# One tile of layer 1's expert mixer: its u rows gathered, its v products kept dense; gelu of blocks done ahead placed one block later

## The chip, the cores and the metric

One core of a Trainium2 chip runs the kernel. The metric is the device time of one execution in microseconds (us), from the first to the last instruction and the little that lies around them; less is better. PE is the matrix engine (TensorE), PEld its weight loads, DVE VectorE, ACT ScalarE, POOL GpSimd; SP issues most of the DMAs, ACT and POOL some. Each engine takes its instructions in the order in which they stand.

## What is computed

Two layers over 512 latent tokens and 256 context tokens of 1024 numbers. Each layer has a token mixer (state space in layer 0, attention in layer 1) and then a PEER mixer. Layer 1 gives results for the 512 latent tokens alone. The change is about PEER:

```
def peer_route(t, w_q, keys):
    q = (t @ w_q).reshape(n_tok, PEER_HEADS, 2, PEER_DK // 2)
    s = einsum('thsd,hsnd->thsn', q, keys)
    sv, si = top_k(s, PEER_TOPK)
    cand = sv[:, :, 0, :, None] + sv[:, :, 1, None, :]
    cv, ci = top_k(cand.reshape(...), PEER_TOPK)
    ...
    return e.reshape(n_tok, -1), softmax(cv).reshape(n_tok, -1)

act = gelu(einsum('td,tkd->tk', hb, u_tab[ib])) * gb
out = einsum('tk,tkd->td', act, v_tab[ib])
```

So each token picks 8 x 16 = 128 of 16384 experts; for each picked expert it takes the product with a row of u, a gelu, a gate, and adds that multiple of a row of v.

## The kernel before

Tokens lie in tiles of 128: tiles 0 and 1 are context, 2 to 5 are latent. There are two ways to do PEER for a tile.

**Gathered** (`gather`): for each of the 128 picks, POOL gathers one row of peer_u per token into a `row` buffer [128, 1024] (five buffers, so up to four fetched ahead), and DVE multiplies it by the token and sums (`row<-row,m`, a row sum). After 128 rows ACT does the gelu, DVE multiplies by the gates, and 128 rows of peer_v follow, each added by DVE to f (an f row).

**Dense**: all 16384 experts in 128 blocks of 128, for all tokens of the dense tiles at once. Per block: U is loaded, split into high and low parts (`Uh` by ACT, `Ul` by DVE), 24 u products give s_ps (block's experts x tokens), ACT applies the gelu (`ge`), DVE multiplies by the gate matrix of the block (`Gt`), the result is split into A, and 18 v products (three tiles) add A times the split block of peer_v (`W`, `Wh`, `Wl`) to accumulators held in PSUM. Gate matrices are built first: `gate_matrix` makes one-hot pairs e and o on DVE and ACT for 8 tokens at a time, PE multiplies them (g_ps), ACT copies the products into `stage`, and slabs go to memory (`gm`), from which `Gt` is loaded for 8 blocks at once.

In layer 0 the tiles 2 to 5 are dense and 0, 1 gathered. In layer 1 the tiles 4, 2, 3 are dense and tile 5 is gathered: 384 columns in each u product, three tiles in the v products (`dense_held`).

Some blocks' u part is done ahead, while tokens are still routed (`ahead`): 40 blocks in layer 0, 48 in layer 1 (three of every eight). Their gelu goes to memory (`ged`) and comes back in the dense stretch.

The order comes from generators that `merge` takes turns with by a count of estimated time (`yield` gives it: 5.2 * NT / 4 for a block, R1 = 3.0 for a row of layer 1), and from a scheduler underneath that may move instructions on an engine. Main streams of a `merge` end it; those in `side=` go on later. In layer 1 one `merge` runs output projection, queries and routing, with the work ahead and the gate matrices at its side; then `peer` merges the rest of the gate matrices and the work ahead with the gather at its side; then `dense_held` with the gather. `keep_in_program_order` pins an instruction. `spare` is the pool of the W buffers. Names in the prediction: m is the tile's tokens, idx its picks, rt the routing result, act the 128 activations per token.

## Time and profile before

| what | us |
|---|---|
| median of 3 runs (4092.92 to 4105.87) | 4102.02 |
| the profiled execution, whole time | 4107.66 |
| the profiled execution, span from first to last instruction | 4105.9 |
| PE busy in the span | 3719.0 |
| DVE busy | 3068.7 |
| ACT busy | 1450.2 |
| POOL busy | 1238.6 |

A busy PE is a modelled figure, since matmuls overlap; a pitch (start of one to start of the next) tells more of what a matmul costs. The mean granted clock of TensorE was 0.956 of full speed, two levels taken together. The rows further down come from this one execution.

### The profile page before, as it was taken

What the parts mean: (1) busy time and instruction counts of PE and PEld (TensorE: products, weight loads), DVE (VectorE), ACT (ScalarE), POOL (GpSimd) and SP (SyncE); (2) the same over time, 40 slices, a digit from 0 to 9 for tenths busy, and PEclk for the clock granted to TensorE, in tenths of its full rate; (3) what the DMA queues carried; (4) which work ended last, traced back from release to release, by engine and by line L of the source; (5) the groups of instructions that cost most, each with busy time, mean ns of one, the idle gap of its engine ahead of it and who ended that gap; (6) DMA issues with size and microseconds to landing.
All of it is one profiled execution on the core that took longest, in us unless ns stands there. A gap on an engine that the chain in (4) does not pass through costs nothing.

```text
span 4105.9 us, 52738 instructions
## 1 busy us (share of the span) xinstructions
PE 3719.0 (91%) x18955; PEld 3031.4 (74%) x18955; DVE 3068.7 (75%) x6143; ACT 1450.2 (35%) x2527; POOL 1238.6 (30%) x940
## 2 busy tenths in 40 slices
PE   6759999888689999999999989998887899999998
PEld 3537768677667878778888855568887788888887
DVE  9784387976867788888898844438977677777764
ACT  1321123366632232232332243323466333333332
POOL 5743000022412455556555300000011344444410
PEclk7879999899999999999999999999999999999999
DMA  5457234377888899999999820144477889888873
GB/s 182 134 176 247 80 131 152 96 241 249 293 311 290 291 338 352 337 354 330 342 338 346 301 98 3 44 169 140 123 234 247 317 327 334 318 320 321 328 271 102
DMA packets 380007, 986.06 MB, mean 240 GB/s; under 512 B 64992, under 2 KB 145376, under 8 KB 375136
## 3 DMA queue, kind: packets, MB, share of 16 engines
q1 hardware_dynamic: 198688, 501.34, 35.4%
q0 software_dynamic: 110592, 402.70, 27.4%
q10 hardware_dynamic: 70464, 78.65, 5.5%
q8 instruction: 149, 2.44, 0.2%
q14 instruction: 114, 0.93, 0.1%
HBM read 892.28 MB, written 90.21 MB: 239 GB/s over the span
## 4 chain that ended last, share of the span: by engine, by line
PE 57%; DVE 14%; issue 12%; DMA 7%; POOL 6%; ACT 3%; SPq 0%; POOLq 0%; ACTq 0%; DVEq 0%
PE s_ps L1111 20%; PE acc L1180 8%; PE acc L1255 8%; POOL row L1323 5%; PE qp L920 3%; PE op L791 3%; DMA U<-in_peer_uT 3%; DMA row<-in_peer_v,idx 2%; PE g_ps L1076 2%; PE zp L762 2%; DVE Ul L306 1%; PE op_mla L1560 1%; DVE w L645 1%; PE yp L697 1%; DMA row<-in_peer_u,idx 1%
## 5 line engine op out<-in xcount | busy, mean ns | idle before, releaser
L1111 PE MATMUL s_ps<-Hs,Uh 128*128 128x512 f32 (+1 forms) x4096 | 1187.4, 371 | 13.5 <-ACT Uh L305 13.5
L1323 POOL DMA_INDIRECT row<-in_peer_u,idx x384 | 528.8, 1377 | 2025.2 <-DVE row L1330 1148.2
L1111 PEld LDWEIGHTS s_ps<-Hs,Uh 128*128 128x128 f32 x4096 | 763.1, 190 | 116.2 <-ACT Uh L305 18.7
L1111 PE MATMUL s_ps<-Hs,Ul 128*128 128x512 f32 (+1 forms) x2048 | 759.6, 371 | 27.2 <-DVE Ul L306 27.1
L1255 PE MATMUL acc<-Ws,A 128*128 128x512 f32 x2976 | 689.1, 393 | 37.5 <-ACT A L305 21.4
L1255 PEld LDWEIGHTS acc<-Ws,A 128*128 128x128 f32 x2976 | 564.3, 190 | 160.6 <-ACT A L305 21.9
L1323 POOL DMA_INDIRECT row<-in_peer_v,idx x384 | 502.9, 1310 | 516.8 <-DVE f L1335 460.7
L306 DVE TENSOR_TENSOR Ul<-U,Uh 128x1024 fp32r<-128x1024 f32 x256 | 312.0, 1219 | 281.8 <-ACT Uh L305 273.6
L1335 DVE SCALAR_TENSOR_TENSOR f<-row,act,f 128x1024 f32<-128x1024 f32 x381 | 487.1, 1278 | 33.8 <-DMA row<-in_peer_v,idx 32.2
L1330 DVE SCALAR_TENSOR_TENSOR row<-row,m 128x1024 f32<-128x1024 f32 x384 | 461.0, 1218 | 42.7 <-DMA row<-in_peer_u,idx 41.7
L1111 PEld LDWEIGHTS s_ps<-Hs,Ul 128*128 128x128 f32 x2048 | 389.5, 190 | 82.3 <-DVE Ul L306 35.3
L305 ACT CAST Uh<-U 128x1024 fp32r<-128x1024 f32 x256 | 268.0, 1050 | 500.0 <-DMA U<-in_peer_uT 454.4
L1180 PE MATMUL acc<-Wh,A 128*128 128x512 f32 x1536 | 426.6, 391 | 12.2 <-ACT A L305 12.2
L1076 PE MATMUL g_ps<-o,o 128*128 128x128 f32 x1792 | 240.3, 293 | 114.5 <-ACT o L1059 72.1
L1180 PEld LDWEIGHTS acc<-Wh,A 128*128 128x128 f32 x1536 | 288.3, 188 | 66.7 <-ACT A L305 12.6
L1114 ACT ACTIVATE ge<-s_ps 128x512 f32<-128x512 f32 (+1 forms) x256 | 138.8, 543 | 556.4 <-PE s_ps L1111 551.1
L1076 PEld LDWEIGHTS g_ps<-o,o 128*128 128x128 f32 x1792 | 229.7, 206 | 126.2 <-ACT o L1059 124.5
L305 ACT CAST A<-ge 128x512 fp32r<-128x512 f32 (+1 forms) x256 | 144.6, 565 | 309.0 <-DVE ge L1236 227.1
L305 ACT CAST Ws<-W 128x512 fp32r<-128x512 f32 x256 | 152.1, 619 | 264.3 <-DMA W<-in_peer_v 217.7
L1180 PE MATMUL acc<-Wl,A 128*128 128x512 f32 x768 | 237.5, 390 | 0.0
L306 DVE TENSOR_TENSOR Ws<-W,Ws 128x512 fp32r<-128x512 f32 x256 | 174.3, 684 | 56.0 <-ACT Ws L305 55.7
L306 DVE TENSOR_TENSOR A<-ge,A 128x512 fp32r<-128x512 f32 (+1 forms) x256 | 158.5, 620 | 54.2 <-ACT A L305 53.7
(340 smaller groups left out, 4780.3 us busy)
## 6 DMA issues: line engine op xcount, KB each, us to landing
U<-in_peer_uT SPq DMA_DIRECT2D x256, 512.0 KB
W<-in_peer_v SPq DMA_DIRECT2D x256, 256.0 KB
W<-in_peer_v SPq DMA_DIRECT2D x128, 512.0 KB
gm<-stage ACTq DMA_DIRECT2D x28, 2048.0 KB
ada_wt<-in_ada_w SPq DMA_DIRECT2D x96, 512.0 KB
Gt<-gm SPq DMA_DIRECT2D x16, 2048.0 KB
Gt<-gm SPq DMA_DIRECT2D x16, 1536.0 KB
wq<-in_peer_w_q SPq DMA_DIRECT2D x40, 512.0 KB
```

The lines of the kernel that those rows point to most:

```text
L305: self.nc.scalar.copy(out=hi, in_=x)
L306: lo_eng.tensor_tensor(out=lo, in0=x, in1=hi.bitcast(F32), op=ALU.subtract)
L791: nc.tensor.matmul(out=op, lhsT=y(i, k), rhs=W, start=(k == 0), stop=(k == KD - 1))
L920: PE.matmul(out=st["p"][:, h % 2, i * 128:(i + 1) * 128], lhsT=W[:, k, :], rhs=st[i][:, k, :], start=(k == 0), stop=(k == KD - 1))
L1076: PE.matmul(out=gp[:, t, :], lhsT=o[1][:, t4 * 4 + t, :], rhs=o[0][:, t4 * 4 + t, :], start=True, stop=True)
L1111: PE.matmul(out=sp, lhsT=x[:, k, :], rhs=self.Hs[:, y, k, :], start=(n == 0), stop=(n == 3 * KD - 1))
L1114: S.activation(out=ge, in_=sp, func=AF.Gelu)
L1180: PE.matmul(out=acc[d][hf], lhsT=A[b][:, x, c], rhs=Ws[y][:, hf * 512:(hf + 1) * 512], start=(b == 0 and n == 0), stop=(b == NB - 1 and n ...
L1255: PE.matmul(out=acc[hf][d], lhsT=A[b][:, x, c], rhs=Ws[:, y], start=(j == 0 and n == 0), stop=(j == SB - 1 and n == 2))
L1323: GP.indirect_dma_start(out=r, out_offset=None, in_=tab, in_offset=bass.IndirectOffsetOnAxis(ap=ik[:, k:k + 1], axis=0), element_offset=l ...
L1330: x = V.scalar_tensor_tensor(out=r, in0=r, scalar=1.0, in1=m, op0=ALU.mult, op1=ALU.mult, accum_out=act[:, k:k + 1])
L1335: x = V.scalar_tensor_tensor(out=f, in0=r, scalar=act[:, k:k + 1], in1=f, op0=ALU.mult, op1=ALU.add)
```

## The change

In layer 1, tile 4 becomes half gathered: its picks of peer_u are gathered (128 more row gathers and row sums), its activations go through gelu and gates as for a gathered tile, but instead of gathering rows of v the product takes the gate's place in tile 4's routing result, so that its "gate matrix" holds finished activations. In the dense stretch the u products then cover tiles 2 and 3 alone (`utiles`, 256 columns), and A's part for tile 4 is split straight from Gt. The v products stay at three tiles. Tile 4 is routed first (order 4, 5, 2, 3, before 5, 4, 2, 3), its gate matrix is built last (2, 3, 4, before 4, 2, 3), and the gather is at the side of layer 1's first merge too.

In both layers, the gelu of a block done ahead and its store are issued after the products of the next block (`behind`). The spare pool has four buffers everywhere; in layer 1 it had three. Hs holds the columns of `utiles` alone.

```diff
     def spare(self, shape, name, dt=F32):
-        return self.pool.tile(shape, dt, tag="spare", bufs=max(3, len(self.tiles)), name=name)
+        return self.pool.tile(shape, dt, tag="spare", bufs=4, name=name)
...
-    def peer_setup(self, l, dense, gather):
+    def peer_setup(self, l, dense, gather, half=()):
...
+        self.tiles, self.gathered, self.half = dense, gather, half
+        self.utiles = [ti for ti in dense if ti not in half]
+        self.rts = {}
...
-        self.Hall = self.big([128, 2, KD, T_LAT], "Hs", F32R)
-        self.Hs = self.Hall[:, :, :, T_LAT - len(self.tiles) * 128:]
+        self.Hs = self.big([128, 2, KD, len(self.utiles) * 128], "Hs", F32R)
...
+        if ti in self.half:
+            self.rts[ti] = rt
+            self.gat[ti] = self.m[ti], gate, idx
+            return
...
-        for ti in self.tiles:
+        for ti in self.utiles + list(self.half):
             while ti not in self.routed:
                 yield 1.0
             yield from self.gate_matrix(ti)
...
+        behind = []
+
+        def gelu(n, sp):
+            ge, x = self.dense_ge(sp)
+            self.tc.keep_in_program_order(x)
+            self.nc.scalar.dma_start(out=self.ged[n], in_=ge)
+
         def work(i, Us):
-            self.nc.scalar.dma_start(out=self.ged[i], in_=self.dense_u(Us))
+            behind.append((i, self.dense_s(Us)))
+            if len(behind) > 1:
+                gelu(*behind.pop(0))
             self.n_done = i + 1
             return 5.2 * NT / 4
...
+        gelu(*behind.pop())
...
         def work_u(b, x):
             ge = x if b in self.early else self.dense_u(x)
-            gv = ge.rearrange("p (d g t) -> p d g t", d=NT, g=4)
-            V.tensor_tensor(out=gv, in0=gv, in1=Gt[b // SB][:, :, :, b % SB, :], op=ALU.mult)
+            gv = ge.rearrange("p (d g t) -> p d g t", d=NU, g=4)
+            G = Gt[b // SB][:, :, :, b % SB, :]
+            V.tensor_tensor(out=gv, in0=gv, in1=G[:, NT - NU:], op=ALU.mult)
             A[b] = self.t4([128, 2, TD], "A", F32R)
-            self.split(A[b][:, 0], A[b][:, 1], ge, V)
-            return 0.0 if b in self.early else 5.2 * NT / 4
+            if TG:
+                hi, lo = (A[b][:, x, 0:TG].rearrange("p (d g t) -> p d g t", g=4, t=32) for x in range(2))
+                self.split(hi, lo, G[:, 0:NT - NU], V)
+            self.split(A[b][:, 0, TG:], A[b][:, 1, TG:], ge, V)
+            return 0.0 if b in self.early else 5.2 * NU / 4
...
             for ph, tab in ((0, a["peer_u"]), (1, a["peer_v"])):
+                if ph and ti in self.half:
+                    break
...
-                    V.tensor_tensor(out=act, in0=act, in1=gk, op=ALU.mult)
+                    V.tensor_tensor(out=gk if ti in self.half else act, in0=act, in1=gk, op=ALU.mult)
+            if ti in self.half:
+                self.routed[ti] = self.rts[ti]
+                continue
...
-        order = gather + dense
+        order = gather + [ti for ti in dense if ti not in half]
...
-        merge(scaled(pipeline(steps, LT), FA), chain(*(self.route(ti) for ti in order)), side=(self.aheads, scaled(self.gates, FG1)))
+        merge(scaled(pipeline(steps, LT), FA), chain(*(self.route(ti) for ti in order)),
+              side=(self.gathering, self.aheads, scaled(self.gates, FG1)))
...
-        self.mla([4, 2, 3], [5])
+        self.mla([4, 2, 3], [4, 5], [4])
```

Where the instructions stand, first on DVE at the end of layer 1's gate matrices (e and o are the one-hot pair, `row,act<-row,m` a row sum, Ul and Wl the low parts of a split). Before, up to the first Wl of the dense stretch:

```order
L306 TENSOR_TENSOR Ul<-U,Uh 128x1024
L1054 TENSOR_TENSOR e<-iota_68,iT 128x2048
L1062 TENSOR_TENSOR o_24236<-e,gT 128x768
L1330 SCALAR_TENSOR_TENSOR row,act<-row,m 128x1024
L1054 TENSOR_TENSOR e<-iota_68,iT 128x2048
L1062 TENSOR_TENSOR o_24260<-e,gT 128x768
L1330 SCALAR_TENSOR_TENSOR row,act<-row,m 128x1024 x3
L306 TENSOR_TENSOR Ul<-U,Uh 128x1024
L1330 SCALAR_TENSOR_TENSOR row,act<-row,m 128x1024 x4
L306 TENSOR_TENSOR Wl<-W,Wh 128x1024
```

After, from the last one-hot pair of tile 3 to the first of tile 4 (`rt<-act,rt` puts the finished activations into the routing result):

```order
L1358 SCALAR_TENSOR_TENSOR row,act<-row,m 128x1024
L1060 TENSOR_TENSOR e<-iota_68,iT 128x2048
L1068 TENSOR_TENSOR o_24002<-e,gT 128x768
L1358 SCALAR_TENSOR_TENSOR row,act<-row,m 128x1024 x80
L1370 TENSOR_TENSOR rt<-act,rt 128x128
L1358 SCALAR_TENSOR_TENSOR row,act<-row,m 128x1024
L1060 TENSOR_TENSOR e<-iota_68,iT 128x2048
L1068 TENSOR_TENSOR o_24315<-e,gT 128x768
```

Eighty row sums of tile 4 now stand in one piece between the last pair of tile 3 and the first of tile 4.

Second on ACT in layer 0's work ahead (ge is the gelu of a block, Uh the high part of a later block's split, o the one-hot casts, stage the copies of gate products). Before:

```order
L305 CAST Uh<-U 128x1024
L1080 DMA gm_2818<-stage 128x16x256
L1059 CAST o_6626<-e 128x1024
L1065 ACTIVATE o_6628<-e,gT 128x128 x2
L1114 ACTIVATE ge<-s_ps 128x512
L1078 COPY stage<-g_ps 128x128x4
L1059 CAST o_6646<-e 128x1024
L1065 ACTIVATE o_6648<-e,gT 128x128 x2
L1126 DMA ged_2854<-ge 128x512
```

After, at the same place:

```order
L305 CAST Uh<-U 128x1024
L1114 ACTIVATE ge<-s_ps 128x512
L1086 DMA gm_2818<-stage 128x16x256
L1142 DMA ged_2854<-ge 128x512
L1065 CAST o_6623<-e 128x1024
L1071 ACTIVATE o_6625<-e,gT 128x128 x2
L1065 CAST o_6643<-e 128x1024
L1071 ACTIVATE o_6645<-e,gT 128x128 x2
L1084 COPY stage<-g_ps 128x128x4 x2
```

The gelu moved up behind the cast Uh, and it is now that of the block before; two casts of o follow it ahead of the stage copies.

Third on DVE at the end of the program (`f<-row,act,f` is an f row of tile 5, `f<-acc` the start of a dense tile's epilogue). Before:

```order
L306 TENSOR_TENSOR Wl<-W,Wh 128x1024
L1164 TENSOR_TENSOR ge<-ge,Gt 128x384
L306 TENSOR_TENSOR A<-ge,A 128x384
L1363 TENSOR_TENSOR f<-acc_24477,m_31481 128x512
L1363 TENSOR_TENSOR f<-acc_24478,m_31481 128x512
L1366 SCALAR_TENSOR_TENSOR f<-h,f 128x1024
```

After:

```order
L1187 TENSOR_TENSOR ge<-ge,Gt 128x256
L306 TENSOR_TENSOR A<-ge,A 128x256
L1363 SCALAR_TENSOR_TENSOR f<-row,act,f 128x1024 x10
L1394 TENSOR_TENSOR f<-acc_24829,m_32137 128x512
L1363 SCALAR_TENSOR_TENSOR f<-row,act,f 128x1024
L1394 TENSOR_TENSOR f<-acc_24830,m_32137 128x512
L1396 TENSOR_TENSOR f<-f,m_32108 128x1024
L1397 SCALAR_TENSOR_TENSOR f<-h,f 128x1024 x2
```

The f rows of tile 5 now reach past the last A; in the order before, all of them stand ahead of it.

## Rows read from the trace of the kernel before

**Rows 1.** Busy time by stretch: us, each engine (instructions), PEclk, DMA share, GB/s
```profile
2000.00:2100.00 100.00, 100.00 (x437) 81.71 (x437) 90.79 (x114) 29.09 (x44) 56.82 (x45) 1.00 0.94 337
3700.00:3900.00 200.00, 196.47 (x956) 173.48 (x955) 156.96 (x167) 69.88 (x96) 90.16 (x61) 1.00 0.89 324
```

**Rows 2.** Chain that ended last: start us, us, what (xcount)
```profile
2806.05 12.67 PE s_ps L1111 x72
...
3183.20 15.87 DMA gm<-stage
...
3207.45 6.69 PE acc L1180 x18
...
3471.57 16.34 PE acc L1180 x72
...
4074.70 6.60 PE acc L1180 x29
```

**Rows 3.** Instructions on a tile: ns min/median/max, first and last start
```profile
L306 DVE TENSOR_TENSOR Ul<-U,Uh x48: 1203/1224/1226, 2804.5 to 3184.2; 128x1024 fp32r<-128x1024 f32 x48
...
L1021 DVE TENSOR_TENSOR rt<-oh x8: 279/281/292, 2821.6 to 2989.3; 128x128 f32<-128x128 bf16 x8
...
L1062 DVE TENSOR_TENSOR o<-e,gT x48: 937/958/959, 2875.2 to 3177.7; 128x768 f32<-128x768 bf16 x48
...
L306 DVE TENSOR_TENSOR A<-ge,A x19: 550/557/563, 3960.3 to 4076.4; 128x384 fp32r<-128x384 f32 x19
```

**Rows 4.** Busy time from 2800 to 3000 us, summed
```profile
sum 200.00, PE 169.04 PEld 160.92 DVE 186.46 ACT 91.03 POOL 4.70; mean PE 33.81 PEld 32.18 DVE 37.29 ACT 18.21 POOL 0.94
```

**Rows 5.** Timeline of PE in the attention: start us, us, what
```profile
2563.94 0.29 PE L1536 MATMUL sp_mla<-knT,qnT 128*128 128x256 f32 x1
2564.06 0.28 PE L1537 MATMUL sp_mla<-krT,qs 128*128 128x256 f32 x1
```

**Rows 6.** Timeline of DVE, layer 0's work ahead, its end
```profile
1087.28 1.22 DVE L1054 TENSOR_TENSOR e<-iota,iT 128x2048 bf16<-128x2048 bf16 x1
...
1089.48 1.22 DVE L1330 SCALAR_TENSOR_TENSOR row<-row,m 128x1024 f32<-128x1024 f32 x1
...
1092.82 1.22 DVE L1330 SCALAR_TENSOR_TENSOR row<-row,m 128x1024 f32<-128x1024 f32 x1
...
1120.59 1.23 DVE L1330 SCALAR_TENSOR_TENSOR row<-row,m 128x1024 f32<-128x1024 f32 x1 [0.72 <-DMA row<-in_peer_u,idx]
...
1122.21 1.23 DVE L1330 SCALAR_TENSOR_TENSOR row<-row,m 128x1024 f32<-128x1024 f32 x1 [0.39 <-DMA row<-in_peer_u,idx]
...
1123.83 1.23 DVE L1330 SCALAR_TENSOR_TENSOR row<-row,m 128x1024 f32<-128x1024 f32 x1 [0.39 <-DMA row<-in_peer_u,idx]
```

**Rows 7.** Timeline of DVE, opening of layer 1
```profile
2999.97 1.22 DVE L1330 SCALAR_TENSOR_TENSOR row<-row,m 128x1024 f32<-128x1024 f32 x1
...
3189.88 0.08 DVE L1330 DVE_READ_ACCUMULATOR row<-row,m 128x1 f32 x1
```

**Rows 8.** DMA queue of gathered rows: packets, MB, share of 16 engines
```profile
q0 software_dynamic: 110592, 402.70, 27.4%
```

**Rows 9.** Timeline of POOL, same stretch as rows 6
```profile
1107.68 1.68 POOL L1323 DMA_INDIRECT row<-in_peer_u,idx  x1 [1.67 <-DVE row L1330]
1109.66 0.94 POOL L1323 DMA_INDIRECT row<-in_peer_u,idx  x1 [0.30 <-issue]
1110.91 1.50 POOL L1323 DMA_INDIRECT row<-in_peer_u,idx  x1 [0.30 <-issue]
```

**Rows 10.** Timelines of ACT and PE, layer 0's work ahead; [idle before <-releaser]
```profile
943.59 0.60 ACT L1114 ACTIVATE ge<-s_ps 128x512 f32<-128x512 f32 x1 [4.98 <-PE s_ps L1111]
...
945.69 5.61 PE L1076 MATMUL g_ps<-o,o 128*128 128x128 f32 x32 [2.13 <-ACT o L1059]
```

**Rows 11.** Waits from 660 to 1130 us: us in total, times, longest
```profile
DVE Ul L306 <- ACT Uh L305: 66.2, 19, 9.0
...
PE g_ps L1076 <- ACT o L1059: 44.0, 30, 6.3
```


## What the change does to the time, predicted before it ran

> **What bounds the kernel now.** I read the busy time by stretches first, then the chain that ended last, then the waits. The reader should see three kinds of stretch. From about 3207 us to the end, the stretch that multiplies by peer_v and by peer_u (call it the dense stretch of layer 1), PE is busy 98% of the time with DVE near 78% and DMA at a 0.89 share [rows 1]. PE sets the time there: the chain alternates s_ps pieces (u products) and acc pieces (v products) from 3207.45 to 4081.30 [rows 2], 873.9 us. Between 2804.5 and 2989.5, while tokens are routed (the first Ul row at 2804.5, the last rt row at 2989.3 [rows 3]), DVE is the busiest engine (186.5 of 200 us) and PE is not the limit (169.0) [rows 4]. Between 2989.5 and 3207.45 the gate matrices are built; PE, ACT and DVE wait for each other, and the stretch closes with the write of gm (15.87 us) and the loads behind it [rows 2]. I call the last two stretches together the opening of layer 1. The change takes work from PE in the dense stretch and puts work on DVE in the opening.
>
> **Part 1, narrower u products.** Each of 128 blocks has 24 products of 384 columns; they become 256 columns. The pitch of a 384-column product is 12.67/72 = 0.176 us [rows 2]. A product of this type with 256 columns stands in the attention part: starts 2563.94 and 2564.06, so 0.120 us [rows 5]. 80 of the blocks lie in the dense stretch: 80 x 24 x (0.176 - 0.120) = 107.5 us. The other 48 are done ahead, in the opening; their 48 x 24 x 0.056 = 65 us lie beside DVE, which binds there, and bring nothing. The v products stay: 128 x 18 at 16.34/72 = 0.227 us [rows 2] = 523 us. PE's own sum for the dense stretch goes from 338 + 523 = 861 to 230 + 523 = 753 us. It took 873.9, so 13 us were lost to late inputs. After the change everything else has to come in less time: in bytes 80 u blocks, 128 v blocks and 242 gathered rows of 128 x 1024 floats (0.524 MB each), 16 gate slabs of 1.57 MB and 48 stored gelus of 0.13 MB, together 267 MB; in 773 us that is 346 GB/s. In layer 0 PE stayed 100% busy with DMA at 337 GB/s, a 0.94 share, and DVE at 91 of 100 us [rows 1], so I only raise the loss from 13 to 20 us; the fourth W buffer helps here. Dense stretch: 773 us, **-101 us**. Below nothing this term can't go unless the pitch does not fall.
>
> The Trainium skill (Perfetto Trace Analysis, section Identifying the Most-Contended Engine) judges TensorE's headroom by the share of time that it loads weights rather than by matmul busy time. That share is 173.5 of 200 us here [rows 1], and the change removes no load; by the rule the stretch could not fall below 0.867 x 873.9 = 758 us, 5 us over my 753. The rows at 0.120 us each have a weight load of their own, so the trace does not bear the floor out [rows 5].
>
> **Part 2, 128 more row gathers.** In the order of the changed kernel the row sums of tile 4 stand on DVE as follows: 29 before the routing ends, 19 among the one-hot pairs of tiles 2 and 3, then 80 in an unbroken run, and then the gate matrix of tile 4 with 14 rows of tile 5. During the run nothing is left for PE: all but three blocks of the work ahead are in front of it, and tile 4's gate products need its result. DVE's prices: an e/o pair takes 2.20 us (1087.28 to 1089.48), a pair with a row 3.34 us (1089.48 to 1092.82), so a row costs 1.14 us when it has landed [rows 6]; an Ul reads the same amount as a row, and I take 1.14 for it.
> Routing: 185 us now. Added are 29 rows (33.1) and 13 more Ul that fall here (14.8), and three pairs leave (-6.6): **+41 us**. DVE had 13.5 of 200 us free [rows 4], so 28 to 41.
> From there to the first acc product: 217.9 us now. After: 19 pairs with a row, 7 without, 7 Ul = 87 us of DVE work. In the kernel before, a mixed stretch with 37 pairs, 32 rows and 19 Ul took 190 us (2999.97 to 3189.88 [rows 7]) for a DVE sum of 37 x 2.20 + 51 x 1.14 = 140, 1.36 times as long; pairs and rows without u blocks ran without gaps [rows 6]. With few u blocks in it I take 100 (87 to 118). The run: DMA's price of a row is 0.274 x 4105.9 / 768 = 1.465 us of all 16 engines [rows 8]; POOL could issue one in 1.25 us (1109.66 to 1110.91) [rows 9]; the nearest rows, three row sums with nothing between them, have pitches of 1.62 us, each waiting for its DMA while gm is written [rows 6]. I take 1.5, nearer to DMA's price because gm is soon out of the way: 80 x 1.5 = 120 us (100 to 130). Then 4 us for act, transposes and iT, and 14 x 3.34 + 2 x 2.20 = 51 us. Closing, from the last o row (3177.7 plus 0.96) to the first acc: 29 us, as before [rows 2, 3]. Together 304 against 218: **+86 us**.
>
> **Part 3, the end.** Last A at 4076.4, end at 4105.9 [rows 3]: 29.5 us, in which DVE waits 4.9 us for PE (4081.30) and then does three epilogues in 24.6. In the new order eleven f rows follow the last A (16 us at 1.5 each, in place of the 4.9), then a fourth epilogue, of which I count 8 us (a third of 24.6): **+19 us**. The m5 row is loaded into a buffer that one of the last rows frees; I leave its few us in the range.
>
> **Part 4, gelu behind.** ACT waits for PE before ge, once for 4.98 us, and o casts stand behind it; PE then waits 2.13 us for ACT's o [rows 10]. With the gelu of the block before in that place, ACT does not stop there. This acts in layer 0 (part 2 already counts DVE alone in layer 1). The most that PE can get back directly is its 44.0 us of waits for ACT's o, the most for DVE its 66.2 us of waits for Uh [rows 11]; the least is nothing, since stage copies still wait for products that stand behind s_ps. I take half of the 44: **-20 us**. The wider spare pool costs memory only; in layer 0 it was four already.
>
> **Sum.** Against the profiled execution: 4105.9 - 101 + 41 + 86 + 19 - 20 = 4131 us of span, +25. That execution took 4107.66 us, 5.6 above the median of the runs (4102.02). So 4102 + 25 = **4127 us**. With the bounds of part 2 and a dense loss of 13 to 35 us, the forecast's own range is 4095 to 4155.
>
> **Rivals.**
> *The gelu was the lock (faster).* If the waits for ge hold the whole layer 0 stretch of gate matrices and u blocks, it shrinks to DVE's own work: the 66.2 us of waits for Uh vanish less some 3 that remain, so 63 instead of 20: 4127 - 43 = 4084. It ends faster than before once layer 0 gives more than 57. For it: ACT's 4.98 us wait and PE's 2.13 behind it [rows 10]. Against: where no u block stood between the pairs DVE was already full at 3.34 us a pair [rows 6], and PE and ACT have nearly as much work as DVE.
> *The run is held by POOL (slower).* POOL's issue took 1.68 us plus 0.30 while DVE worked, 1.98 per row (1107.68 to 1109.66) [rows 9]. If that holds in the run, it takes 158 us: 4127 + 38 = 4165. Against: issues of 0.94 us stand there too [rows 9].
> The Trainium skill (GPSIMD Engine Reference, section 1, Specifications) says that GpSimd shares its SBUF interfaces with VectorE and contends with instructions that have two SBUF inputs, which every row sum is. By that rule the 1.98 is the run's pitch and this rival's time holds; the rows agree only where DVE is full, so it gets a small chance.
> *The dense stretch is fed late (slower).* If DMA gives no more than the 324 GB/s at which the dense stretch ran [rows 1], 267 MB take 824 us instead of 773: 4127 + 51 = 4178. Against: layer 0's 337 GB/s with PE at 100%.
> *It does not do what it says (slower).* If 256-column products keep the pitch of 384, the 107.5 us don't come: 4127 + 107 = 4234. Rows 5 speak against it.
>
> **How the numbers follow.** Forecast 0.47, gelu 0.25, POOL 0.12, fed late 0.11, no shorter product 0.03, 0.02 for others. 0.3% of 4102 is 12.3 us, about what a measurement can tell from no change: faster is below 4089.7, slower above 4114.3. The forecast spreads some 17 us to either side, so it gives 0.01 faster, 0.11 same, 0.35 slower; the gelu rival 0.16 and 0.09; all the others are slower, 0.28. Faster 0.17, same 0.20, slower 0.63. The range takes in the gelu rival down to its bound and both middle rivals: 4072 to 4180.
>
> **What would show it.** In the changed profile: s_ps products at 0.12 us pitch and a dense stretch near 773 us; the first acc product some 107 us later than 3207.45 (127 less layer 0's 20); a stretch of about 120 us with PE nearly idle, DVE doing row sums with waits for row DMA, POOL issuing every 1.5 us; granted clock below 1.0 in it; ACT's waits for s_ps before ge gone in the work ahead, and layer 0's dense stretch starting 20 us earlier. I am wrong if the run is much shorter than 100 us, if layer 0 gains over 50, or if PE is below 95% busy in the dense stretch.

## The result, and the profile after

The changed kernel takes 4161.34 us (median of 3 runs, 4144.76 to 4164.95) where the kernel before takes 4102.02: a ratio of 1.0138, 95% interval 1.0089 to 1.0188. It is slower, as forecast, by 59 us where 25 were forecast. The profiled execution spans 4159.6 us, 53.7 more than before; the other 5.6 us of the 59.3 are the distance of the profiled execution of before from its median.

The stages, from the first and last starts of the same instructions in both traces (before: [rows 3] and [rows 2]; after: the rows below):

| stage | before | after | moved | forecast |
|---|---|---|---|---|
| to the first Ul of layer 1 | 2804.5 | 2796.9 | -7.6 | -20 |
| routing (first Ul to last rt) | 184.8 | 220.1 | +35.3 | +41 |
| last rt to first acc product | 218.1 | 315.5 | +97.4 | +86 |
| dense stretch (first acc to last A) | 869.0 | 776.0 | -93.0 | -101 |
| last A to the end | 29.5 | 51.1 | +21.6 | +19 |
| span | 4105.9 | 4159.6 | +53.7 | +25 |

The instructions on single tiles give the borders (ns least/median/most, first and last start in us):

```profile
L306 DVE TENSOR_TENSOR Ul<-U,Uh x47: 1193/1217/1268, 2796.9 to 3064.8; 128x1024 fp32r<-128x1024 f32 x47
...
L1023 DVE TENSOR_TENSOR rt<-oh x8: 275/282/284, 2814.7 to 3017.0; 128x128 f32<-128x128 bf16 x8
...
L1068 DVE TENSOR_TENSOR o<-e,gT x48: 939/958/959, 2954.3 to 3304.0; 128x768 f32<-128x768 bf16 x48
...
L306 DVE TENSOR_TENSOR A<-ge,A x36: 406/417/424, 3901.0 to 4108.5; 128x256 fp32r<-128x256 f32 x36
```

They answer to [rows 3]. The chain that ended last (start, us, what) shows the closing of the opening and the new pace of the dense stretch, beside [rows 2]:

```profile
3309.73 15.50 DMA gm<-stage
3325.25 6.91 DMA Gt<-gm
3332.53 6.50 PE acc L1206 x18
3339.03 2.88 PE s_ps L1124 x24
3341.91 4.12 PE acc L1206 x18
```

24 u products of 256 columns take 2.88 us, 0.120 each, as read ahead from [rows 5]; a block of v products takes 4.12. PE's own sum is 80 x 2.88 + 128 x 4.12 = 758 us. The stretch takes 776 us up to the last A, but PE still multiplies behind it: the last start among the v products shows that they end at 4118.0, 785.5 us after the first, 27 more than the sum.

```profile
L1206 PE MATMUL acc<-Wh,A x1536: 387/389/795, 3332.5 to 4117.6; 128*128 128x512 f32 x192
```

The busy time by stretches (us of each engine, instructions; PEclk, DMA share, GB/s) shows routing, a piece of the unbroken run of rows, and the dense stretch:

```profile
2797.00:3017.00 220.00, 163.21 (x1158) 153.61 (x1158) 215.89 (x827) 85.07 (x133) 38.99 (x34) 0.88 0.64 203
```
```profile
3200.00:3240.00 40.00, 0.00 (x0) 0.00 (x0) 30.00 (x51) 0.00 (x0) 31.44 (x25) 0.50 0.89 318
```
```profile
3332.00:4108.00 776.00, 758.90 (x4181) 662.58 (x4182) 623.93 (x935) 299.24 (x542) 334.46 (x230) 0.99 0.91 333
```

DVE is all but full in routing (215.9 of 220 us). In the unbroken run of rows (from here on: the run) PE does nothing, and its granted clock is 0.50, the lower level of 1.2 GHz. In the dense stretch PE stands still for 17 of 776 us while DMA moves 333 GB/s.

The run is a single wait in PE's list (us in total, times, longest), and the queue of gathered rows has grown from 768 to 896 rows at the same price, 0.317 x 4159.6 / 896 = 1.472 us of all DMA engines each (1.465 from [rows 8]):

```profile
PE tr_ps L1046 <- DVE rt L1370: 131.9, 1, 131.9
```
```profile
q0 software_dynamic: 129024, 469.82, 31.7%
```

The 315.5 us from the last rt to the first acc product divide at 3125.2 (first row of the run), 3259.2 (rt from act) and 3304.0 (last o): a mixed stretch of 108, the run with 134, tile 4's gate pairs 45, the closing 28.5.

In layer 0 the waits of ACT between 660 and 1142 us show what the moved gelu did, first of before, then of after:

```profile
ACT ge L1114 <- PE s_ps L1111: 114.6, 34, 5.3
...
ACT stage L1078 <- PE g_ps L1076: 23.7, 58, 1.7
```
```profile
ACT stage L1084 <- PE g_ps L1082: 67.3, 68, 12.2
...
ACT ge L1114 <- PE s_ps L1124: 20.5, 6, 5.0
```

The wait before ge has fallen from 114.6 to 20.5 us, and a good part of it stands before the stage copies now (67.3 us for 23.7). The first acc product of layer 0 moved from 1147.0 to 1141.9 us, by 5.

The end, in the chain:

```profile
4116.30 6.11 DMA row<-in_peer_v,idx
4122.50 1.29 DVE f L1363
4124.26 6.81 DMA h<-hd
4131.07 2.34 DVE f L1397 x2
```

The last gathered row lands at 4122.4, 14 us after the last A; then h is loaded, then the epilogues run.

### The profile page after: what moved, and what is told of

Its sections match the earlier page's. It is cut to its first block, busy times and chain, and to the rows that moved or that the text cites. A ratio compares the mean times of both kernels' runs of the same rounds, so it can differ in the third digit from the quotient of the medians.

```text
span 4159.6 us, 53685 instructions
## 1 busy us (share of the span) xinstructions
PE 3570.8 (86%) x18963; PEld 2879.0 (69%) x18963; DVE 3202.8 (77%) x6528; ACT 1438.3 (35%) x2653; POOL 1412.2 (34%) x1068
## 4 chain that ended last, share of the span: by engine, by line
PE 45%; issue 19%; DVE 17%; DMA 8%; POOL 8%; ACT 2%; SPq 1%; POOLq 0%; DVEq 0%; ACTq 0%
PE s_ps L1124 12%; POOL row L1351 7%; PE acc L1206 7%; PE acc L1281 7%; DMA U<-in_peer_uT 4%; PE op L791 3%; PE qp L922 3%; DMA row<-in_peer_v,idx 2%; DVE Ul L306 2%; PE zp L762 2%; DVE row L1358 1%; PE op_mla L1591 1%; DVE rw L952 1%; DVE tk_tmp L950 1%; DVE w L645 1%
## 5 line engine op out<-in xcount | busy, mean ns | idle before, releaser
L1351 POOL DMA_INDIRECT row<-in_peer_u,idx x512 | 683.4, 1335 | 2061.0 <-DVE row L1358 1112.7
L1124 PE MATMUL s_ps<-Hs,Uh 128*128 128x512 f32 (+1 forms) x4096 | 1044.8, 346 | 20.7 <-ACT Uh L305 20.7
L1124 PEld LDWEIGHTS s_ps<-Hs,Uh 128*128 128x128 f32 x4096 | 725.4, 195 | 122.3 <-ACT Uh L305 25.0
L1124 PE MATMUL s_ps<-Hs,Ul 128*128 128x512 f32 (+1 forms) x2048 | 712.5, 348 | 57.2 <-DVE Ul L306 57.0
L1351 POOL DMA_INDIRECT row<-in_peer_v,idx x384 | 522.8, 1362 | 503.0 <-DVE f L1363 447.0
L1358 DVE SCALAR_TENSOR_TENSOR row<-row,m 128x1024 f32<-128x1024 f32 x512 | 616.5, 1219 | 73.8 <-DMA row<-in_peer_u,idx 71.1
L1124 PEld LDWEIGHTS s_ps<-Hs,Ul 128*128 128x128 f32 x2048 | 398.6, 195 | 112.9 <-DVE Ul L306 66.5
L305 ACT CAST A<-ge 128x512 fp32r<-128x512 f32 (+1 forms) x256 | 130.5, 512 | 294.2 <-DVE ge L1262 202.2
L1114 ACT ACTIVATE ge<-s_ps 128x512 f32<-128x512 f32 (+1 forms) x256 | 124.9, 488 | 277.1 <-PE s_ps L1124 272.3
L306 DVE TENSOR_TENSOR A<-ge,A 128x512 fp32r<-128x512 f32 (+1 forms) x256 | 140.9, 551 | 34.3 <-ACT A L305 34.0
```

Of the source, the lines that this page charges most:

```text
L305: self.nc.scalar.copy(out=hi, in_=x)
L306: lo_eng.tensor_tensor(out=lo, in0=x, in1=hi.bitcast(F32), op=ALU.subtract)
L1114: return ge, self.nc.scalar.activation(out=ge, in_=sp, func=AF.Gelu)
L1124: PE.matmul(out=sp, lhsT=x[:, k, :], rhs=self.Hs[:, y, k, :], start=(n == 0), stop=(n == 3 * KD - 1))
L1351: GP.indirect_dma_start(out=r, out_offset=None, in_=tab, in_offset=bass.IndirectOffsetOnAxis(ap=ik[:, k:k + 1], axis=0), element_offset=l ...
L1358: x = V.scalar_tensor_tensor(out=r, in0=r, scalar=1.0, in1=m, op0=ALU.mult, op1=ALU.mult, accum_out=act[:, k:k + 1])
```

## The experiments

Stage times are read from each kernel's trace as in the table above; times are medians against the kernel before on the same chip (4099 to 4102 us).

| kernel | time | ratio, 95% | layer 0 ahead* | opening | dense | end |
|---|---|---|---|---|---|---|
| before | 4102.02 | | 482.5 | 402.9 | 869.0 | 29.5 |
| after | 4161.34 | 1.0138 (1.0089 to 1.0188) | 479.0 | 535.6 | 776.0 | 51.1 |
| gelu_only | 4111.91 | 1.0028 (1.0019 to 1.0038) | 483.1 | 414.6 | 866.2 | 29.5 |
| half_only | 4183.23 | 1.0204 (1.0185 to 1.0222) | 483.0 | 549.0 | 782.4 | 50.4 |
| rows48 | 4035.79 | 0.9839 (0.9821 to 0.9856) | 482.0 | 403.1 | 791.4 | 47.2 |
| tail_pace | 4188.52 | 1.0226 (1.0200 to 1.0251) | 479.6 | 533.8 | 831.0 | 27.3 |
| half_products | 4157.89 | 1.0142 (1.0123 to 1.0161) | 478.6 | 534.0 | 781.1 | 49.6 |
| half_bytes | 4138.03 | 1.0097 (1.0078 to 1.0116) | 480.2 | 531.9 | 780.0 | 27.5 |
| half_width | 4134.67 | 1.0098 (1.0074 to 1.0121) | 479.1 | 515.3 | 773.0 | 49.6 |
| early_rows | 4138.87 | 1.0100 (1.0082 to 1.0117) | 479.7 | 506.7 | 779.4 | 50.1 |
| spare3 | 4158.31 | 1.0139 (1.0122 to 1.0156) | 481.9 | 534.2 | 777.2 | 50.2 |
| pool_ul | 4085.59 | 0.9953 (0.9935 to 0.9970) | 471.8 | 404.1 | 867.9 | 29.9 |
| early_pool | 4136.69 | 1.0087 (1.0056 to 1.0118) | 468.3 | 522.8 | 782.1 | 50.1 |
| pool_l0 | 4081.27 | 0.9955 (0.9939 to 0.9972) | 463.9 | 399.5 | 870.4 | 29.6 |

*From layer 0's first Ul, on whichever engine, to its first acc product. The opening runs from layer 1's first Ul to its first acc product, the dense stretch from there to the last A.

**The gelu by itself.** gelu_only is the kernel before with this part of the change alone; half_only the changed kernel without it.

```
+        def gelu(n, sp):
+            ge, x = self.dense_ge(sp)
...
         def work(i, Us):
-            self.nc.scalar.dma_start(out=self.ged[i], in_=self.dense_u(Us))
+            behind.append((i, self.dense_s(Us)))
+            if len(behind) > 1:
+                gelu(*behind.pop(0))
```

> The kernel before with the gelu placed behind the next block's products, and nothing else. Theory A (the wait only changed its place: ACT stops at the stage copies, which stand behind the same products on PE, so DVE and PE get next to nothing back): ACT's waits before ge go from 100 us between 660 and 1110 us to about 10, its waits before stage copies rise from 24 to about 67, and the last Ul of layer 0 comes 5 us earlier; 0 to 8 us in all, time 4094 to 4102. Theory B (the forecast's 20 us are there, and the changed kernel lost some of them elsewhere): about 4082, with layer 0's first acc product near 1127 instead of 1147 us. Theory C (the gelu was the lock): 4040 to 4060.

Measured: 4111.91, slower than before by 0.28%. Layer 0's stretch is 483.1 us against 482.5: nothing gained. The opening of layer 1 grew by 11.7. Theory A has the mechanism, but not the sign; B and C are out. In layer 0, between 660 and 1146 us, first ACT's and then DVE's wait read:

```profile
ACT stage L1078 <- PE g_ps L1076: 70.8, 68, 11.1
```
```profile
DVE Ul L306 <- ACT Uh L305: 64.1, 18, 7.8
```

ACT waits 71 us before stage copies (23.7 before), and DVE's wait for Uh stays at 64 where it was 66.2 [rows 11]. In the opening, from the last rt to the first acc, the same wait of DVE rises from 59.3 to 71.8 us.

half_only, the other way round:

```
-            self.tc.keep_in_program_order(x)
...
-            if len(behind) > 1:
+            if behind:
                 gelu(*behind.pop(0))
...
-        gelu(*behind.pop())
```

> The changed kernel with the gelu straight behind its own products again, so the half gather alone. If the two parts are independent and the gelu is worth 5 to 8 us, 4166 to 4170 us against 4161, and the first acc product of layer 0 at 1147 us as in the kernel before, with an opening of layer 1 of about 535 us and a dense stretch of about 776. Rival: the opening is what gains from the gelu behind (the work ahead runs there too); then the opening gets longer than 540 us.

Measured: 4183.23, 22 above the changed kernel. In the spans: 3 us up to layer 0's first acc product, 13 in the opening, 6 in the dense stretch. The rival was right: the opening gains from the gelu behind when the half gather is there, and loses without it. Ten of the 13 us lie in routing (230.1 against 220.1), where DVE's waits for Uh fall from 7.8 us to 1.5; how the rest comes about, and why the gelu behind costs 12 us without the half gather and gains 22 with it, no run shows.

**What paces layer 0's stretch.** half_products takes half of PE's u products away there:

```
-            behind.append((i, self.dense_s(Us)))
+            behind.append((i, self.dense_s(Us, KD if l else KD // 2)))
```

> The changed kernel with 12 instead of 24 u products for each of the 40 blocks that layer 0 does ahead (half of the sum over the 1024 features is left out there, so the output lacks it). It takes some 24 x 40 x 0.113 = 109 us of work from PE between 660 and 1142 us and nothing from DVE, ACT or DMA. Theory A (the stretch is paced by PE's order: stage copies and, behind them, o casts wait for gate products that stand behind a block's u products, wherever the gelu is): layer 0's first acc product comes 40 to 90 us earlier than 1142, and ACT's waits before stage copies fall from 67 us to under 30. Rival (DVE with its 98% at the start and 70 to 83% later sets the time): it comes less than 15 us earlier. The rest of the kernel keeps its time.

Measured: 478.6 us where the changed kernel has 479.0. The two windows, changed kernel and half_products:

```profile
660.00:1142.00 482.00, 374.47 (x2136) 320.85 (x2134) 383.91 (x1042) 252.69 (x441) 96.46 (x65) 0.93 0.64 216
```
```profile
660.00:1142.00 482.00, 297.35 (x1629) 251.71 (x1628) 384.32 (x1023) 253.82 (x443) 93.04 (x64) 0.82 0.64 213
```

77 us of PE's busy time went (less than the 109 of the products, while the granted clock fell from 0.93 to 0.82), and the stretch did not move: PE does not pace it, and Theory A fell. PE's waits only changed their length (g_ps for ACT's o 93 us, from 43.6). DVE's 384 us and its 61 us of waits for Uh stayed. So the next runs changed DVE's list instead: pool_ul lets POOL do the Ul of every second block of the work ahead of the kernel before.

```
-        yield from pipeline([(lambda b=b: self.dense_u_prep(l, b, self.nc.vector), ...
+        yield from pipeline([(lambda b=b, i=i: self.dense_u_prep(l, b, self.nc.gpsimd if i % 2 else self.nc.vector), ...
```

> The kernel before, in which POOL does the Ul of every second block of the work ahead, in both layers (20 of 40 and 24 of 48; 24 and 29 us taken from DVE), and nothing else. It asks what paces these stretches, since halving PE's u products moved layer 0's stretch by less than 1 us. Theory A (DVE with what it waits for sets both): first acc product of layer 0 after 455 to 470 us instead of 482.5, opening of layer 1 375 to 390 instead of 403, time 4050 to 4080. Rival (POOL's own subtraction takes several us, and stands behind row issues that wait for DVE, so that u products come late): no stretch gets shorter, 4100 or more.

Measured: 4085.59, 0.47% faster than before, but only half of theory A: layer 0's stretch shrank by 11 us for 24 us of Ul taken from DVE; the opening of layer 1 did not shrink (404.1 us for 402.9). POOL's groups in layer 0 (busy us, mean ns):

```profile
L1323 POOL DMA_INDIRECT row<-in_peer_u,idx x68 | 102.2, 1503 | 472.4 <-DVE rw L949 301.8 <-DVE row L1330 152.7 <-PE qp L920 7.9
L306 POOL TENSOR_TENSOR Ul<-U,Uh 128x1024 fp32r<-128x1024 f32 x20 | 53.3, 2667 | 139.2 <-ACT Uh L305 91.1 <-DVE Ul L306 29.0 <-DVE rw L947 15.7
```

POOL needs 2.67 us for an Ul that takes DVE 1.22. pool_l0 takes two of three blocks in layer 0, and none in layer 1:

```
+        self.nc.gpsimd if l == 0 and i % 3 else self.nc.vector
```

> The kernel before, in which POOL does the Ul of two of three blocks that layer 0 does ahead (26 of 40), and of none in layer 1. If DVE still paces layer 0's stretch, 26 Ul less of 1.22 us give 12 to 20 us instead of the 11 of pool_ul (first acc product after 462 to 470 us), time 4078 to 4086. Rival (POOL's own row issues and Ul of 2.67 us now come late and u products wait): 472 us or more, time 4086 or more.

Measured: 463.9 us, 19 less than before, for 26 Ul or 32 us taken from DVE's list; time 4081.27, 0.45% faster than before (0.9955, 0.9939 to 0.9972). This kernel beats both.

But DVE's busy time did not fall. The stretch in the kernel before and in pool_l0, then DVE's wait for Uh in pool_l0 (66.2 us before [rows 11]):

```profile
664.00:1147.00 483.00, 377.77 (x2115) 322.25 (x2113) 381.89 (x1022) 255.18 (x441) 94.84 (x65) 0.92 0.65 215
```
```profile
661.00:1125.00 464.00, 373.90 (x2116) 320.48 (x2114) 385.12 (x998) 253.08 (x440) 160.91 (x91) 0.92 0.67 223
```
```profile
DVE Ul L306 <- ACT Uh L305: 38.2, 6, 9.4
```

The timelines of POOL and of DVE in pool_l0 show what took the 32 us up again:

```profile
901.36 2.45 POOL L306 TENSOR_TENSOR Ul<-U,Uh 128x1024 fp32r<-128x1024 f32 x1
```
```profile
898.16 1.22 DVE L1330 SCALAR_TENSOR_TENSOR row<-row,m 128x1024 f32<-128x1024 f32 x1
...
901.51 3.39 DVE L1330 SCALAR_TENSOR_TENSOR row<-row,m 128x1024 f32<-128x1024 f32 x1
```

A row sum that begins during POOL's Ul takes 3.4 us instead of 1.2: it ends about 1.1 us after the Ul does. Eight row sums of the stretch do this, some 17 us in all, and other DVE instructions with two inputs (e, oh) bring the total to some 33. So what got shorter is not DVE's work but its standing still: 28 us less of waits for Uh, since the Ul that wait no longer stand in DVE's list. That the order on DVE, with its waits, paces this stretch fits all three runs; what makes Uh late was not tested.

**The run.** rows48 leaves out the last 80 row sums of tile 4:

```
+            nk = 48 if ti in self.half else 128
+            if nk < 128:
+                V.memset(act, 0.0)
...
-                ... for k in range(128)], NROW - 1)
+                ... for k in range(nk)], NROW - 1)
```

> The changed kernel with only the first 48 row sums of tile 4; the last 80, those in the unbroken run, are left out (their activations are set to zero), so the output lacks them. Theory A (the run lies on the path from end to end, with nothing beside it): the time falls by the run's 133 us, to 4025 to 4035, and the first acc product comes near 3200 instead of 3332. Rival: something else ends just behind the run (the write of tile 3's gates, loads, the rest of the work ahead), so that less than 100 us go; the first acc product then comes later than 3230.

Measured: the opening is 403.1 us, 132.5 shorter, and the first acc product comes at 3199.2. The run of 134 us lies on the path from end to end. The time fell by 125.5 us only, since the dense stretch grew from 776 to 791, for which no run gives the cause.

What sets the run's pace, 80 rows with starts 1.68 us apart? half_width gathers half as many bytes with as many issues, and its row sums are half as wide:

```
+                    w = D // 2 if ti in self.half and k >= 48 else D
-                    GP.indirect_dma_start(out=r, out_offset=None, in_=tab,
+                    GP.indirect_dma_start(out=r[:, 0:w], out_offset=None, in_=tab.rearrange("r (h d) -> (r h) d", d=w) if w < D else tab,
```

> The changed kernel in which the 80 row gathers and row sums of tile 4's unbroken run take 512 elements instead of 1024 (other elements than the reference wants, half of each sum is left out): the same number of POOL issues, half the bytes, half the DVE time. Theory A (DMA sets the run's 1.66 us per row): the run goes from 133 us to POOL's least pitch of 0.94 + 0.30 = 1.24 us, 95 to 108 us, time 4130 to 4138. Rival (POOL sets it, since in the run it issues with 0.30 us between issues and rarely waits for DVE): the run stays above 120 us, time above 4148.

Measured: the run takes 113.5 us (3121.4 to 3234.9), between both theories; row sums start 1.42 us apart. POOL's group in the run, changed kernel and half_width:

```profile
L1351 POOL DMA_INDIRECT row<-in_peer_u,idx x78 | 97.1, 1245 | 34.6 <-issue 19.2 <-DVE row L1358 15.4
```
```profile
L1352 POOL DMA_INDIRECT row<-in_peer_u,idx x77 | 85.5, 1111 | 27.1 <-issue 21.3 <-DVE row L1360 5.8
```

POOL alone, with the time between issues, needs (97.1 + 19.2)/78 = 1.49 us a row in the changed kernel, and 1.39 with half the bytes, where DMA's share is 0.69 and cannot be the limit. The remaining 0.2 of the 1.68 are POOL's waits for DVE, which has itself waited for DMA. So POOL sets most of the pitch, with DMA close behind (1.472 us a row); the halved bytes, with the row sums that are halved with them (0.69 instead of 1.22 us), took 20 of 134 us.

Why is a mean issue 1.25 us when the shortest take 0.94? The trace of early_rows, the next run, tells it best, since DVE is full there with instructions of two kinds. POOL's and DVE's timelines:

```profile
2898.63 0.94 POOL L1351 DMA_INDIRECT row<-in_peer_u,idx  x1 [0.60 <-DVE rw L948]
2901.67 1.87 POOL L1351 DMA_INDIRECT row<-in_peer_u,idx  x1 [2.10 <-DVE rw L951]
```
```profile
2898.75 0.28 DVE L949 FIND_INDEX8 rw<-rw,scr 128x8 uint32<-128x128 f32 x1
...
2901.52 1.21 DVE L306 TENSOR_TENSOR Ul<-U,Uh 128x1024 fp32r<-128x1024 f32 x1
```

Beside the searches of the routing (MAX8, FIND_INDEX8, MATCH_REPLACE8) an issue takes 0.94 us, beside an Ul 1.87: it ends 0.8 us after the Ul. Over that routing the 27 issues whose first 0.93 us fall on searches and the like take 0.93 to 0.95 us each; the 34 whose first 0.93 us fall on instructions with two inputs (Ul, row sum, the one-hot steps of routing) take a median of 1.68; 16 fall on both kinds, one on neither. In the run, too, an issue that begins while DVE stands still takes 0.94 us, and one that begins beside a row sum up to 1.98. So the row sums lengthen the very issues that feed them, and half_width's shorter issues (none above 1.31 us) fit its shorter row sums; what the bytes took by themselves was not separated.

early_rows brings the rows forward, 94 of them ahead of the run instead of 48:

```
-              side=(self.gathering, self.aheads, ...
+              side=(scaled(self.gathering, 0.4), self.aheads, ...
```

> The changed kernel with a row counted at 0.4 of its time while layer 1's tokens are routed, so that 94 instead of 48 row sums of tile 4 stand ahead of the run, which keeps 34. Theory A (a row costs 1.66 us in the run, where DMA or POOL sets the pitch, and only DVE's 1.2 us where DVE is the limit): routing gets longer by about 47 x 1.2 = 56 us, the run shorter by 46 x 1.66 = 76, the opening 15 to 25 us shorter, time 4136 to 4146. Rival (rows among the routing hold up more than their own DVE time, since routing steps stand behind rows that have not landed): the opening does not get shorter, time 4160 or more.

Measured: routing 269.6 us (+49.5), the run 57 (34 rows), the opening 506.7, 29 us shorter than the changed kernel's; time 4138.87. Theory A, a little better than forecast. In routing DVE is all but full:

```profile
2860.00:3060.00 200.00, 121.80 (x793) 115.63 (x794) 199.35 (x688) 60.21 (x95) 75.38 (x60) 0.78 0.77 250
```

44 more row sums stand ahead of the last rt, so a row costs 49.5/44 = 1.13 us there, against 1.68 in the run. Even so the half gather stays 1.0% slower than before: 128 rows at that price alone cost some 144 us, and the dense stretch gives back 93.

early_pool adds pool_ul's edit to this kernel.

> The kernel of early_rows with the same edit: POOL does the Ul of every second block ahead. Theory A: DVE is full through layer 1's routing here (199 of 200 us), so each Ul taken away there counts whole: opening 480 to 490 instead of 507, layer 0 as in pool_ul, time 4095 to 4115. Rival: POOL has 1.26 us issues of rows in the same stretch, and each Ul on POOL delays rows and products; no gain, 4135 or more.

Measured: 4136.69, no gain. Layer 0 gave 11 us, as in pool_ul, and routing took them back (285.5 us against 269.6). On POOL an Ul of 2.37 us stands in one queue with 112 row issues of 1.26 us. The trace shows that DVE did not get the Ul's time back here either: it is busy 279.6 of 285 us in routing, where early_rows has 266.9 of 270, because 13 row sums that meet an Ul of POOL take 2.2 to 3.8 us instead of 1.22. One of them, POOL's line and then DVE's:

```profile
2996.74 2.37 POOL L306 TENSOR_TENSOR Ul<-U,Uh 128x1024 fp32r<-128x1024 f32 x1
```
```profile
2996.88 3.32 DVE L1358 SCALAR_TENSOR_TENSOR row<-row,m 128x1024 f32<-128x1024 f32 x1
```

**The end and the dense stretch.** tail_pace puts all f rows ahead of the last A:

```
-        merge(... self.dense(l), self.gathering)
+        merge(... self.dense(l), scaled(self.gathering, 0.93 if self.half else 1.0))
```

> The changed kernel with a gathered row counted at 0.93 of its time in the dense stretch of layer 1, so that all f rows stand ahead of the last A on DVE and none behind it. Theory A (the end got longer because eleven rows and a fourth epilogue stand behind the last A): end minus last A goes from 51 us back to about 30, the dense stretch stays near 776, time 4135 to 4145. Rival (the rows cost the same wherever they stand, since DMA is the limit there): the dense stretch grows by what the end loses, 15 us or more, and the time stays at 4155 to 4165.

Measured: the end is 27.3 us, 24 less, but the dense stretch 831, 55 more; 4188.52 in all. The rival holds, and the loss is larger than it said: 11 rows more in the stretch are 11 x 1.47 = 16 us of DMA. half_bytes has the same order and every second row of tile 5 left out, the one before it used twice:

```
+                    if l and ti not in self.half and k % 2:
+                        return prev.pop()
```

> The kernel of tail_pace, in which every second gathered row of tile 5 is left out and the row ahead of it is used twice, so the output is not the reference's; DVE has the same instructions in the same order, POOL and DMA have 128 rows (67 MB) less, nearly all of them in the dense stretch. Theory A (DMA feeds the dense stretch late: tail_pace lost 55 us there at 0.85 to 0.93 DMA share and 46 of 50 us PE): the dense stretch goes from 831 to 755 to 770 us, near PE's own 753, PE above 98% busy, time 4105 to 4125. Rival (the row instructions ahead of the splits on DVE hold the blocks up, not the bytes): the dense stretch stays above 800 us and the time above 4150.

Measured: 780.0 us. The dense stretches of tail_pace and of half_bytes:

```profile
3323.00:4154.00 831.00, 778.68 (x4193) 675.65 (x4194) 645.88 (x958) 301.83 (x548) 333.68 (x237) 0.97 0.87 319
```
```profile
3328.00:4108.00 780.00, 762.79 (x4192) 665.57 (x4193) 645.58 (x958) 301.69 (x548) 164.80 (x116) 0.98 0.74 258
```

DVE does the same in both (646 us); with the rows' transfers and issues halved, 51 of the 55 us come back. In tail_pace PE stands still for 52 us (17 in the changed kernel), and its products take 17 us longer up to its last one (785.7 us busy for 768.9), at a granted clock of 0.97 instead of 0.99: a late input is paid for twice. Theory A is half right only: in half_bytes PE is busy all the time up to 3680 us, at 7.0 us a block as its own sum wants it, but beyond that, in the f rows, 46 to 49 of 50 us at a DMA share of 0.65 to 0.76. What it waits for there (ACT's Uh, behind U loads) is hardly for want of bytes, and its cause stays open. Since POOL's issues were halved with the bytes, the two are not told apart here.

spare3 takes the fourth W buffer back:

```
-        return self.pool.tile(shape, dt, tag="spare", bufs=4, name=name)
+        return self.pool.tile(shape, dt, tag="spare", bufs=max(3, len(self.tiles)), name=name)
```

> The changed kernel with three instead of four W buffers in layer 1, as in the kernel before. Theory A (the fourth buffer lets loads run further ahead in a dense stretch that is fed late): without it the dense stretch grows from 776 to 785 to 800 us, time 4170 to 4185. Rival (U, not W, comes late there: ACT waits 312 us for U by DMA, and U has its own buffers): 770 to 782, time 4150 to 4168.

Measured: 777.2 us in the dense stretch, 4158.31: the fourth buffer does nothing. ACT waits for U there, in the changed kernel and in spare3:

```profile
ACT Uh L305 <- DMA U<-in_peer_uT: 311.9, 70, 13.8
```
```profile
ACT Uh L305 <- DMA U<-in_peer_uT: 307.8, 66, 14.0
```

## Why the prediction was right in direction and short in size

The time lies 34 us above the forecast, 6 above the forecast's own range (4095 to 4155) and inside the whole one (4072 to 4180). Of the 34, 28.7 us are terms of the sum (53.7 against 25); the rest is the execution of before.

- **Dense stretch, -93 for -101.** The pitch of 0.120 us was right. The v products were taken at 4.085 us a block and take 4.12, so PE's own sum is 758, not 753. The loss to late inputs was read too small in both kernels, since 4081.30 is not where PE's products end: in the trace of before the last v product starts at 4086.6 and ends 0.39 us later, so 879.5 us stand against a sum of 861, a loss of 18, not 13. In the changed kernel it is 27 (785.5 against 758), not 20; the growth, 9 where 7 were put, is nearly right. The choice between 337 and 324 GB/s was right (333), but close: tail_pace shows the stretch at the edge where a few more rows cost 55 us. That is the "fed late" rival at a pace slightly above this one. The help that the prediction expected of the fourth W buffer is not there (spare3). The v products at the end of the kernel before:

```profile
L1180 PE MATMUL acc<-Wh,A x157: 388/389/399, 3999.7 to 4086.6; 128*128 128x512 f32 x157
```

- **The floor of 758 us by weight loads.** The Trainium skill (Perfetto Trace Analysis, Identifying the Most-Contended Engine) offers the share of weight loads as one measure of TensorE's headroom; that the stretch could not fall below it was the prediction's own reading. The part of half_bytes in which PE never waits runs at 7.0 us a block, which is 758 for the stretch; but this is PE's sum of products, not loads: 24 loads of 194 ns, 4.66 us, pass in 2.88 us of u products, and the loads' busy time fell from 761 to 663 us with as many loads. So the share is no floor here, and that both figures meet at 758 is an accident. One group of loads in the dense stretch (busy us, mean ns):

```profile
L1124 PEld LDWEIGHTS s_ps<-Hs,Uh 128*128 128x128 f32 x1280 | 208.1, 194 | 19.4 <-ACT Uh L305 13.7
```

  1280 loads of 194 ns are 248 us by themselves and 208 in busy time: they overlap each other.
- **Routing, +35 for +41.** DVE's free time took up some of it, as the bound of 28 allowed.
- **Run, +134 for 120.** The step that failed is the pitch, 1.5 us by DMA's price. POOL needs 1.49 of itself, and its waits for DVE add 0.2. The rival with POOL at 1.98 us a row had the right engine and the right mechanism, with every issue counted at its longest: 1.68 us and 0.30 between issues hold only for those that begin beside a DVE instruction with two inputs, the others take 0.94, and the mean in the run is 1.25. The Trainium skill's sentence on SBUF interfaces that GpSimd shares with VectorE (GPSIMD Engine Reference, section 1, Specifications) names just such instructions, and the trace agrees: 0.94 us beside searches, a median of 1.68 beside instructions with two inputs (early_rows). The mean alone hides this: it is 1.25 us in the run and 1.26 in early_rows, where DVE is busy 199 of 200 us, but not with two-input instructions alone.
- **Mixed stretch and gates.** 108 for 100, within its bounds. The 55 us for the gates of tile 4 became 45: of the 14 rows counted there only 9 stand ahead of its last pair (16 x 2.20 + 9 x 1.14 = 45.5). Together with the run this is +97 for +86.
- **End, +22 for +19.** Rows behind the last A and a fourth epilogue, as forecast; the load of h behind the last rows (6.81 us) was not in the sum.
- **Gelu, -5 to -8 for -20.** Here a mechanism failed, not a size. The step took half of PE's 44 us of waits as time got back. half_products shows that PE had spare time in this stretch: 77 us less of its work moved nothing. The waits of an engine that does not set the pace were worth nothing here. gelu_only shows the part alone at +12 us, and half_only shows it at -22 in the changed kernel, mostly in layer 1, where the prediction had put nothing. That -22 comes near the -20 of the sum is luck; the half gather alone costs 84 us (half_only against before), where the sum without this term has 45.

Of the rivals, the gelu as a lock and the product that does not get shorter are out; the POOL rival is right about what holds the run, and its 158 us for it are 24 too many.

## What to carry to other kernels

Before a wait is priced, ask whether its engine paces the stretch, and test it by taking work from that engine: here 77 us less on PE moved nothing, and 26 instructions fewer in DVE's list, with the waits in front of them, moved 19. Before work is moved from DVE to POOL, look at what it will stand beside: in this case the two lengthened each other's instructions, and DVE's busy time did not fall. Trading products for gathered rows takes work from the engine that binds one stretch and puts it on what binds the others; count rows where nothing else can run at their full pitch, and rows beside a full DVE at DVE's price. A stretch that is fed at the rate it uses has no room for a little more: 16 us of extra transfers cost 55.

## What the runs showed that was not expected

- Late inputs cost PE twice: with 35 us more of standing still its products took 17 us more at a lower granted clock (tail_pace, 785.7 us busy against 768.9 up to the last product).
- POOL does a subtraction of 128x1024 in 2.67 us on average (pool_ul; 2.35 at the least) where DVE takes 1.22, and a row sum of DVE that begins meanwhile takes up to 3.4 us in layer 0 (pool_l0) and 3.8 in layer 1 (early_pool). In layer 0 the move was a gain (pool_l0, 19 us), in layer 1 under the half gather a loss (early_pool, 16 us of routing).
- Halving the bytes of a gathered row, and its row sum, shortened its pitch only from 1.68 to 1.42 us: POOL's issue costs 0.94 us at the least, with half the bytes too, more beside a row sum, and 0.25 to 0.3 between issues.
